# The attention of a hybrid encoder layer as one sequence of steps, two stretches on TensorE for a pair of heads in place of four

## The chip, the cores and the metric

The kernel runs on one core of a Trainium2 chip. A core has five engines that work side by side, each from a queue of its own and in order: TensorE (PE) for matmuls, with the loading of its stationary operand shown apart (PEld); VectorE (DVE) and ScalarE (ACT) for elementwise work; GpSimd (POOL); and SyncE (SP), which here only sends DMAs. Matmul results land in PSUM, eight banks of 128 x 512 float32; everything else lives in SBUF. The metric is the device time of one execution in microseconds.

## What is computed

One encoder layer on 512 tokens (a grid of 8 rows x 64 columns) of width 2048, all in float32. The normalised input goes through one projection. Half of its columns feed a gated depthwise convolution (group A), the other half a neighbourhood attention with 16 heads of width 64 (group B); both are normalised, concatenated, projected and added to the input; then follow a gated MLP with a short convolution and a last normalisation. The part that the change touches is the attention:

```python
def neighborhood_attention(q, k, v, rpb):
    ...
    def row_block(r):
        rs = jnp.clip(r - kh // 2, 0, rows - kh)
        k_rows = lax.dynamic_slice_in_dim(kg, rs, kh, axis=1)
        v_rows = lax.dynamic_slice_in_dim(vg, rs, kh, axis=1)
        k_win = k_rows[:, :, col_idx]
        v_win = v_rows[:, :, col_idx]
        q_row = lax.dynamic_index_in_dim(qg, r, axis=1, keepdims=False)
        scores = jnp.einsum("bchd,bicjhd->bchij", q_row, k_win).astype(jnp.float32)
        dr = rs + jnp.arange(kh) - r + (WIN_H - 1)
        bias = rpb_cols[:, dr]
        scores = scores + jnp.transpose(bias, (2, 0, 1, 3))[None]
        p = jax.nn.softmax(scores.reshape(b, GRID_W, h, kh * kw), axis=-1)
        p = p.reshape(b, GRID_W, h, kh, kw).astype(v.dtype)
        return jnp.einsum("bchij,bicjhd->bchd", p, v_win)
```

A token sees all 8 rows and a window of 16 columns.

## The kernel before

**Projection.** `project(n)` computes 128 columns of the projection for all 512 tokens into one PSUM bank. Each weight unit (8 blocks of 128 x 128) is loaded by SP, split by ACT into a rounded part (`whi`, line 125) and by DVE into the rest (`wlo`, line 126), and each block makes three matmuls in `mm3` (lines 136 to 138): 24 matmuls a unit, two units a column block. The text `ORDER` (line 59) says what is projected when: "a" is two blocks of group A (value and gate), "q" is a pair of heads (its queries and its keys), "v" half of the values of all heads.

**Ticks.** Work other than the projection is written as Python generators in two lists, `steps` and `asteps`. After the last matmul of a unit `tick(m)` advances the first generator of each list by one `yield`, and `issue_after` (line 147) keeps the matmuls so issued behind `m` on TensorE. If a generator ends, the next one of its list starts in the same tick. "a" and "q" make four ticks each, the first "v" sixteen, the second none; the output projection `out_half` makes sixteen for each half. The order on the engines is then made by a planner that takes instructions by priority (which follows the program) as their operands and buffers are ready; `pin` holds an instruction behind the one written just before it on its engine. The first matmul of each part is not pinned.

**Attention.** The heads go in pairs, eight of them. A head's tokens are cut into four column blocks of 16 columns x 8 rows (128 queries), each against 32 columns x 8 rows (256 keys). For each pair `attend` has parts that each treat two blocks of both heads:

- `scores(b0)`: four matmuls (line 452; each stands as two records in the trace), operands of 64 rows, the two heads in the two halves of the array's rows; then on DVE the bias table is added (line 462, the table loaded at line 458 by SP) and the maximum taken, on ACT the exponential (467) and the scaling by the reciprocal sum (470). The scores take the one PSUM tile `sc` of two banks.
- `turn()`: eight transposes (line 482) into the two banks `tr`, copied by ACT to SBUF (`pt`, line 486).
- `values(b0)`: eight matmuls (line 495; two records each), the heads in the two halves of the array's columns, into the one bank `po`. After the second call ACT copies `po` out (`ao`, line 512) and the sum of squares is taken.

A generator for each pair runs them: scores(0) in its first tick, nothing in the second, turn and scores(2) in the third, values(0) in the fourth, turn in the fifth, values(2) in the sixth, in which the next pair's scores(0) follows if that pair is already projected.

**Beside and behind it.** `group_a` (in `asteps`, from the fourth pair on) makes the normalisations of group A; it uses the `tr` banks too. When all pairs are done, `norm_b` normalises group B and splits it into `mbh` and `mbl` (lines 169 and 170). `out_half(ma)` projects group A's half and runs while the last pairs are worked off; `out_half(mb)` needs `mbh` and `mbl`. Most SBUF tiles of 128 x 512 come from one pool `t2k` with 73 slots (`NT`).

Of the kernel before, what the change touches and what calls it, by code (L numbers as in the profile page):

```python
# [10 lines left out]
F32 = mybir.dt.float32  # L11
F32R = mybir.dt.float32r
AF = mybir.ActivationFunctionType
# [3 lines left out]
P = 128  # L17
D = 2048
S = 512
# [13 lines left out]
NP_ = HEADS // 2  # L33
# [4 lines left out]
BLK = 16  # L38
# [36 lines left out]
def layer(ctx: ExitStack, tc: tile.TileContext, xT, w_in, w_v, w_out, w_up, w_down, par, g3r, tab, out):  # L75
    nc = tc.nc
# [6 lines left out]
    psa = ctx.enter_context(tc.tile_pool(name="psa", bufs=1, space=bass.MemoryType.PSUM))  # L83
# [9 lines left out]
    def t2(name, dt=F32):  # L93
        return tp.tile([P, S], dt, tag="t2k", name=name)
# [46 lines left out]
    steps, asteps = [], []  # L141
# [31 lines left out]
    def sum_sq(acc, src, first):  # L173
        if first:
            nc.scalar.activation(acc, src, AF.Square)
        else:
            q = t2("sq")
            nc.scalar.activation(q, src, AF.Square)
            nc.vector.tensor_add(acc, acc, q)
# [72 lines left out]
    for step in ORDER:  # L252
        if step == "v":
            i = next(v_)
# [3 lines left out]
        i = next(a_ if step == "a" else q_)  # L258
# [7 lines left out]
    rstd, late = [], []  # L266
# [13 lines left out]
    def project(n):  # L280
        ps = psm.tile([P, S], F32, tag="mm", name="pj")
        for u in range(KD // U):
            w = weights()
            for k in range(U):
                kk = u * U + k
                m = mm3(ps, w, k, xs[kk][0], xs[kk][1], kk == 0, kk == KD - 1)
                if k % TICK == TICK - 1:
                    tick(m)
            while late and rstd:
                late.pop(0)()  # L290
        return ps
# [3 lines left out]
    def project_values():  # L295

        h = len(vts)
        if h == 0:
            both = psa.tile([P, 2, S], F32, tag="sc", name="pv")
            ps = [both[:, 0], both[:, 1]] + [psm.tile([P, S], F32, tag="mm", name="pv") for _ in range(2)]  # L300
        else:
            while late:
                late.pop(0)()
            ps = ([psa.tile([P, S], F32, tag="tr", name="pv", bufs=2)] +
                  [psm.tile([P, S], F32, tag="mm", name="pv") for _ in range(3)])
        for u in range(KD // 2):
            w = weights()
            for c in range(2):
                kk = 2 * u + c
                a = slice(c * S, (c + 1) * S)  # L310
                for i in range(S // P):
                    xh, xl = (x[:, i * P:(i + 1) * P] for x in xs[kk])
                    nc.tensor.matmul(ps[i], xh, w[0][:, a], start=kk == 0, stop=False)  # L313
                    nc.tensor.matmul(ps[i], xh, w[1][:, a], start=False, stop=False)  # L314
                    m = nc.tensor.matmul(ps[i], xl, w[0][:, a], start=False, stop=kk == KD - 1)  # L315
                if h == 0:
                    tick(m)
            while late and rstd:
                late.pop(0)()
        vd = dram.tile([S, S], F32, name=f"vd{h}")  # L320
        for i in range(S // P):
            t = t2("v")
            nc.scalar.activation(t, ps[i], AF.Copy, scale=rcol[:, i:i + 1])
            nc.sync.dma_start(vd[i * P:(i + 1) * P], t)
        by = vd.rearrange("(r c) d -> r c d", c=GW)
        vt = []
        for b in range(NB):
            for ch in range(2):
                vt.append(t2("vt"))
                for r in range(4):  # L330
                    nc.sync.dma_start(vt[-1][r * KW:(r + 1) * KW], by[4 * ch + r, KC0[b]:KC0[b] + KW])
        vts.append(vt)
# [83 lines left out]
    aos = []  # L416
    acc_na = t2("accna")

    def grid(t, c0, w):
        return t.rearrange("p (r c) -> p r c", c=GW)[:, :, c0:c0 + w]  # L420

    def qkv(p):
        got = []
        for j, nm in enumerate("qk"):
            ps = project(2 * NC_ + j * NP_ + p)
            if nm == "q":

                t = t2(nm)
                by = "p (r b c) -> p r b c"
                nc.vector.tensor_mul(t.rearrange("p (b r c) -> p r b c", b=NB, r=WH),  # L430
                                     ps.rearrange(by, b=NB, r=WH), rstd[0].rearrange(by, b=NB, r=WH))
            else:
                t = t2(nm)
                nc.vector.tensor_mul(t, ps, rstd[0])
            got.append(t)
        return got

    def attend(p, q, k):


        hps = [slice(j * DH, (j + 1) * DH) for j in range(2)]
        vt = vts[p * 2 // NP_]
        cols = [slice(p % (NP_ // 2) * P + j * DH, p % (NP_ // 2) * P + (j + 1) * DH) for j in range(2)]
        po = psa.tile([P, S], F32, tag="po", name="po")
        soft = []

        def scores(b0):
            both = psa.tile([P, 2, 2, 2 * P], F32, tag="sc", name="sc")
            for i in range(2):
                b = b0 + i  # L450
                for j, hp in enumerate(hps):
                    m = nc.tensor.matmul(both[:, j, i, :], q[hp, b * P:(b + 1) * P], grid(k, KC0[b], KW)[hp],
                                         start=True, stop=True)
                    if i or j:
                        pin(m)
            for j in range(2):
                tb = t2("tab").rearrange("p (i k) -> p i k", i=2)
                i = nc.sync.dma_start(tb, tab[2 * p + j][:, b0 // 2:b0 // 2 + 2])
                if p == 0:
                    pin(i)  # L460
                s = t2("s").rearrange("p (i k) -> p i k", i=2)
                nc.vector.scalar_tensor_tensor(s, both[:, j], DH ** -0.5, tb, op0=ALU.mult, op1=ALU.add)
                nm = sm.tile([P, 2], F32, tag="nm", name="nm")
                nc.vector.tensor_reduce(nm, s, axis=AX.X, op=ALU.max, negate=True)
                su = sm.tile([P, 2], F32, tag="su", name="su")
                for i in range(2):
                    nc.scalar.activation(s[:, i], s[:, i], AF.Exp, bias=nm[:, i:i + 1], accum_out=su[:, i:i + 1])
                nc.vector.reciprocal(su, su)
                for i in range(2):
                    nc.scalar.activation(s[:, i], s[:, i], AF.Copy, scale=su[:, i:i + 1])  # L470
                soft.append(s)

        pts = []

        def turn():
            pts.clear()
            for j in range(2):
                s = soft.pop(0)
                ps = psa.tile([P, 4, P], F32, tag="tr", name="trp", bufs=2)
                for i in range(2):  # L480
                    for ch in range(2):
                        m = nc.tensor.transpose(ps[:, 2 * i + ch, :], s[:, i, ch * P:(ch + 1) * P], ident)
                        if i or j or ch:
                            pin(m)
                pt = t2("pt").rearrange("p (c k) -> p c k", c=4)
                nc.scalar.activation(pt, ps, AF.Copy)
                pts.append(pt)

        def values(b0):
            for i in range(2):  # L490
                b = b0 + i
                for ch in range(2):
                    for j in (1, 0):
                        hp = hps[j]
                        m = nc.tensor.matmul(grid(po, b * BLK, BLK)[hp], vt[2 * b + ch][:, cols[j]],
                                             pts[j][:, 2 * i + ch, :], start=(ch == 0), stop=(ch == 1))
                        if (i, ch, j) != (0, 0, 1):
                            pin(m)

        scores(0)  # L500
        yield
        yield
        turn()
        scores(2)
        yield
        values(0)
        yield
        turn()
        yield
        values(2)  # L510
        ao = t2("ao")
        nc.scalar.activation(ao, po, AF.Copy)
        aos.append(ao)
        sum_sq(acc_na, ao, p == 0)

    p, n = -1, 0
    for step in ORDER:
        if step == "v":
            project_values()
            continue  # L520
        if step == "a":
            if n < 2:
                with tc.issue_after(last.ins):
                    glu(n)
            else:
                glu(n)
            n += 1
            continue
        p += 1
        steps.append(attend(p, *qkv(p)))  # L530
        if p == NORM_AT:
            asteps.append(group_a())

# [478 lines left out]
```

## Time and profile before

| | |
|---|---|
| median of 3 runs | 2034.68 us (2034.24 to 2035.8) |
| profiled execution | 2034.49 us |
| span of its instructions | 2032.7 us |
| TensorE busy | 2023.2 us (100%) |
| VectorE busy | 1594.4 us (78%) |
| ScalarE busy | 1035.0 us (51%) |
| mean granted TensorE clock | 0.999 |
| attention on TensorE | first scores at 145.0 us, last values at 558.7 us |

Rows of the timeline read: start in us, duration in us, engine, line of the kernel, operation, output tile <- input tiles, shape of the operands, number of instructions merged into the row. Matmuls are pipelined, so the durations of neighbours overlap, and the distance between two starts says more than a duration. Rows of a tile's view give minimum, median and maximum duration in ns, and the first and the last start in us. Rows of waits read: engine and line <- what it waited for: us in total, times, longest.

### The profile page before, as it was taken

The numbers are of one execution on the slowest core, as the hardware profiler recorded it, in microseconds if no ns is written. First come the engines' busy times: TensorE is split into PE (matmuls) and PEld (weight loads), VectorE is DVE, ScalarE is ACT, GpSimd is POOL, SyncE is SP. The second block draws the span as 40 slices with busy tenths as digits, with TensorE's granted clock in tenths as the row PEclk, the third lists the DMA queues.
The fourth block names the chain that finished last, engine by engine and source line by source line (L and its number), as shares of the span: only waits on it lengthen the run. The fifth ranks groups of instructions, "written<-read, shape, count | busy, mean of one in ns | idle before, by whom it ended". The sixth has DMA issues, their size and how long they took to land.

```text
span 2032.7 us, 27622 instructions
## 1 busy us (share of the span) xinstructions
PE 2023.2 (100%) x10546; PEld 1716.7 (84%) x10546; DVE 1594.4 (78%) x1981; ACT 1035.0 (51%) x1530; POOL 141.6 (7%) x174
## 2 busy tenths in 40 slices
PE   9999999999999999999999999999999999999998
PEld 7888888877888998888888888888888888888887
DVE  7798893876577898787877877877787877888886
ACT  7224423476445645555645645545555645545553
POOL 0000000000001000001101111111110110110000
PEclk9999999999999999999999999999999999999999
DMA  6532325325447544456756666656666656766563
GB/s 235 166 104 83 97 92 175 104 83 178 143 143 178 125 129 141 141 151 150 151 136 165 138 154 144 159 134 159 147 152 142 141 133 142 173 160 163 133 191 133
DMA packets 121189, 293.15 MB, mean 144 GB/s; under 512 B 29408, under 2 KB 29920, under 8 KB 121056
## 3 DMA queue, kind: packets, MB, share of 16 engines
q1 hardware_dynamic: 97296, 246.28, 39.5%
q0 software_dynamic: 23040, 44.05, 14.4%
q8 instruction: 83, 1.36, 0.3%
q10 hardware_dynamic: 720, 1.06, 0.1%
q14 instruction: 50, 0.41, 0.1%
HBM read 232.61 MB, written 58.72 MB: 143 GB/s over the span
## 4 chain that ended last, share of the span: by engine, by line
PE 99%; DMA 0%; DVE 0%; ACT 0%; SPq 0%; issue 0%; DVEq 0%
PE pu L695 14%; PE pv L695 11%; PE pd L794 8%; PE pd L796 8%; PE pd L795 8%; PE pu L702 8%; PE pj L136 6%; PE pj L137 6%; PE pv L702 6%; PE pj L138 6%; PE po L136 3%; PE po L138 3%; PE po L137 3%; PE pv L314 1%; PE pv L315 1%; PE pv L313 1%
## 5 line engine op out<-in xcount | busy, mean ns | idle before, releaser
L125 ACT ACTIVATE whi<-raw 128x1024 fp32r<-128x1024 f32 x364 | 383.5, 1054 | 442.1 <-PE pd L796 172.0
L126 DVE TENSOR_TENSOR wlo<-raw,whi 128x1024 fp32r<-128x1024 f32 x364 | 444.3, 1221 | 171.5 <-ACT whi L125 157.1
L695 PE MATMUL pu<-xc,whi 128*128 128x512 f32 x1280 | 344.8, 391 | 0.0
L695 PEld LDWEIGHTS pu<-xc,whi 128*128 128x128 f32 x1280 | 241.2, 189 | 42.3
L695 PE MATMUL pv<-xc,whi 128*128 128x512 f32 x960 | 259.9, 392 | 0.0
L794 PE MATMUL pd<-whi,hh 128*128 128x512 f32 x640 | 249.9, 391 | 0.0
L796 PE MATMUL pd<-whi,hl 128*128 128x512 f32 x640 | 249.4, 390 | 0.0
L795 PE MATMUL pd<-wlo,hh 128*128 128x512 f32 x640 | 249.1, 389 | 0.0
L695 PEld LDWEIGHTS pv<-xc,whi 128*128 128x128 f32 x960 | 181.3, 189 | 30.9
L125 ACT ACTIVATE whi<-ws 128x1024 fp32r<-128x1024 f32 x132 | 139.8, 1059 | 132.3 <-issue 49.3
L136 PE MATMUL pj<-xh,whi 128*128 128x512 f32 x512 | 200.6, 396 | 0.1
L138 PE MATMUL pj<-xh,wlo 128*128 128x512 f32 x512 | 200.3, 391 | 0.0
L137 PE MATMUL pj<-xl,whi 128*128 128x512 f32 x512 | 200.2, 391 | 0.1
L702 PEld LDWEIGHTS pu<-xc,wlo 128*128 128x128 f32 x1280 | 174.6, 190 | 12.5
L702 PE MATMUL pu<-xc,wlo 128*128 128x256 f32 x1280 | 178.5, 282 | 0.0
L371 DVE SCALAR_TENSOR_TENSOR y<-ch,prm,y 128x507 f32<-128x507 f32 (+14 forms) x240 | 171.5, 741 | 3.4
L126 DVE TENSOR_TENSOR wlo<-ws,whi 128x1024 fp32r<-128x1024 f32 x132 | 161.2, 1221 | 4.5 <-ACT whi L125 4.4
L821 POOL DMA_DIRECT2D xq<-pdc x120 | 104.7, 872 | 828.1 <-ACT pdc L819 820.1
L796 PEld LDWEIGHTS pd<-whi,hl 128*128 128x128 f32 x640 | 120.1, 188 | 26.0
L795 PEld LDWEIGHTS pd<-wlo,hh 128*128 128x128 f32 x640 | 120.2, 188 | 25.8 <-DVE wlo L126 0.3
L794 PEld LDWEIGHTS pd<-whi,hh 128*128 128x128 f32 x640 | 120.5, 188 | 22.0
L702 PEld LDWEIGHTS pv<-xc,wlo 128*128 128x128 f32 x960 | 131.0, 190 | 9.4
(188 smaller groups left out, 3169.3 us busy)
## 6 DMA issues: line engine op xcount, KB each, us to landing
raw<-in_w_up SPq DMA_DIRECT2D x176, 512.0 KB, 3.6
raw<-in_w_down SPq DMA_DIRECT2D x88, 512.0 KB, 3.6
xq<-pdc POOLq DMA_DIRECT2D x136, 256.0 KB, 4.9
raw<-in_w_in SPq DMA_DIRECT2D x60, 512.0 KB, 3.8
raw<-in_w_out SPq DMA_DIRECT2D x32, 512.0 KB, 3.7
x<-in_xT SPq DMA_DIRECT2D x32, 256.0 KB, 5.1
raw<-in_w_v SPq DMA_DIRECT2D x16, 512.0 KB, 4.1
tab<-in_tab SPq DMA_DIRECT2D x32, 256.0 KB, 4.2
```

What stands on the lines that cost most here:

```text
L125: i = nc.scalar.activation(hi[:, :n], raw[:, :n], AF.Copy)
L126: j = nc.vector.tensor_sub(lo[:, :n], raw[:, :n], hi[:, :n].bitcast(F32))
L136: nc.tensor.matmul(ps, hi[:, a], mh, start=start, stop=False)
L137: nc.tensor.matmul(ps, hi[:, a], ml, start=False, stop=False)
L138: return nc.tensor.matmul(ps, lo[:, a], mh, start=False, stop=stop)
L371: nc.vector.scalar_tensor_tensor(y[:, a:b], h[:, a + j - PAD:b + j - PAD], prm[:, o + j:o + j + 1], y[:, a:b], op0=ALU.mult, op1=ALU.add)
L695: return nc.tensor.matmul(to, hi[:, a(k)], comb[c][k], start=first and k == 0, stop=k == U - 1, skip_group_check=not first)
L702: nc.tensor.matmul(to[:, H:], lo[:, a(k)], comb[c][k][:, :H], start=False, stop=False, skip_group_check=not first)
L794: nc.tensor.matmul(ps, h, hi, start=start, stop=False)
L795: nc.tensor.matmul(ps, h, lo, start=False, stop=False)
L796: return nc.tensor.matmul(ps, l, hi, start=False, stop=stop)
L821: nc.gpsimd.dma_start(xq[a][i], t, accum_op=ALU.add)
```

## The change

The generator per pair goes. `pair(p, q, k)` only returns the three functions `scores`, `turn` and `values` of a pair, the transposed tiles are kept under their block number, and the closing copy moves into `values(2)`. One generator `attention()` for all pairs takes them from a list `ready`, to which a pair is added when it has been projected. In its ticks stand, with an empty tick after each: turn(0), scores(2) and the values(2) of the pair before; then values(0), turn(2) and, if the next pair is ready, its scores(0). If it isn't, its scores(0) open a stretch of their own as soon as it is, with the values(2) that are still due.

```diff
-    def attend(p, q, k):
+    def pair(p, q, k):
...
-        po = psa.tile([P, S], F32, tag="po", name="po")
-        soft = []
+        soft, pts, po = [], {}, []
...
-        pts = []
-
-        def turn():
-            pts.clear()
+        def turn(b0):
+            pts[b0] = []
...
-                pts.append(pt)
+                pts[b0].append(pt)
 
         def values(b0):
+            if not po:
+                po.append(psa.tile([P, S], F32, tag="po", name="po"))
...
-        scores(0)
-        yield
-        yield
-        turn()
-        scores(2)
-        yield
-        values(0)
-        yield
-        turn()
-        yield
-        values(2)
-        ao = t2("ao")
-        nc.scalar.activation(ao, po, AF.Copy)
-        aos.append(ao)
-        sum_sq(acc_na, ao, p == 0)
+            if b0:
+                ao = t2("ao")
+                nc.scalar.activation(ao, po[0], AF.Copy)
+                aos.append(ao)
+                sum_sq(acc_na, ao, p == 0)
+
+        return scores, turn, values
+
+    ready = []
+
+    def attention():
+
+        late, now = None, None
+        for p in range(NP_):
+            if now is None:
+                while not ready:
+                    yield
+                now = ready.pop(0)
+                now[0](0)
+                if late:
+                    late[2](2)
+                    late = None
+                yield
+                yield
+            scores, turn, values = now
+            turn(0)
+            scores(2)
+            if late:
+                late[2](2)
+            yield
+            yield
+            values(0)
+            turn(2)
+            late, now = now, ready.pop(0) if ready else None
+            if now:
+                now[0](0)
+            yield
+            yield
+        late[2](2)
...
-        steps.append(attend(p, *qkv(p)))
+        ready.append(pair(p, *qkv(p)))
+        if p == 0:
+            steps.append(attention())
```

More of the change, by code (lines that the diff above doesn't have):

```diff
@@ L494, in values @@
                         hp = hps[j]
-                        m = nc.tensor.matmul(grid(po, b * BLK, BLK)[hp], vt[2 * b + ch][:, cols[j]],
-                                             pts[j][:, 2 * i + ch, :], start=(ch == 0), stop=(ch == 1))
+                        m = nc.tensor.matmul(grid(po[0], b * BLK, BLK)[hp], vt[2 * b + ch][:, cols[j]],
+                                             pts[b0][j][:, 2 * i + ch, :], start=(ch == 0), stop=(ch == 1))
                         if (i, ch, j) != (0, 0, 1):
                             pin(m)
-        scores(0)
-        yield
-        yield
-        turn()
-        scores(2)
-        yield
-        values(0)
-        yield
-        turn()
-        yield
-        values(2)
-        ao = t2("ao")
-        nc.scalar.activation(ao, po, AF.Copy)
-        aos.append(ao)
-        sum_sq(acc_na, ao, p == 0)
+            if b0:
[33 more added lines that the diff above has]
+        late[2](2)
     p, n = -1, 0
```

## The prediction

> **What bounds the kernel now.** I read the page first: the busy times and the chain of waits that ended last.
>
> ```profile
> PE 2023.2 (100%) x10546; PEld 1716.7 (84%) x10546; DVE 1594.4 (78%) x1981; ACT 1035.0 (51%) x1530; POOL 141.6 (7%) x174
> ...
> PE 99%; DMA 0%; DVE 0%; ACT 0%; SPq 0%; issue 0%; DVEq 0%
> ```
>
> TensorE is never without work, and 99% of the chain is its own. So a change to the attention counts only through TensorE: by what its instructions cost between the projection's matmuls, or by a wait put into its queue. The profiled execution took 2034.49 us (1.8 us of it outside its span, the same in the changed kernel), and the median of the three runs is 2034.68 us, 0.2 us above that; I add 0.2 at the end.
>
> A busy TensorE doesn't tell what a stretch of attention costs, as matmuls overlap in the records. I take the starts from the timeline of TensorE instead. First the plain pace, then one stretch of each kind, always from the last projection matmul before it to the second one after it (S are scores, line 452; T are the transposes of `turn`, line 482; V are the values, line 495):
>
> ```profile
> 199.64 0.39 PE L137 MATMUL pj<-xl,whi 128*128 128x512 f32 x1
> ...
> 216.87 0.39 PE L138 MATMUL pj<-xh,wlo 128*128 128x512 f32 x1
> 217.18 1.13 PE L452 MATMUL sc<-k,q 64*128 64x256 f32 x8
> 218.25 0.50 PE L136 MATMUL pj<-xh,whi 128*128 128x512 f32 x1
> 218.58 0.40 PE L137 MATMUL pj<-xl,whi 128*128 128x512 f32 x1
> ```
>
> ```profile
> 229.03 0.40 PE L138 MATMUL pj<-xh,wlo 128*128 128x512 f32 x1
> 229.26 1.04 PE L482 MATMUL trp<-ident,s 128*128 128x128 f32 x8
> 230.23 1.14 PE L452 MATMUL sc<-k,q 64*128 64x256 f32 x8
> 231.30 0.50 PE L136 MATMUL pj<-xh,whi 128*128 128x512 f32 x1
> 231.63 0.40 PE L137 MATMUL pj<-xl,whi 128*128 128x512 f32 x1
> ```
>
> ```profile
> 236.66 0.39 PE L138 MATMUL pj<-xh,wlo 128*128 128x512 f32 x1
> 236.98 1.09 PE L495 MATMUL po<-pt,vt 128*64 128x128 f32 x16
> 238.00 0.50 PE L136 MATMUL pj<-xh,whi 128*128 128x512 f32 x1
> 238.34 0.40 PE L137 MATMUL pj<-xl,whi 128*128 128x512 f32 x1
> ```
>
> ```profile
> 243.34 0.40 PE L138 MATMUL pj<-xh,wlo 128*128 128x512 f32 x1
> 243.58 1.04 PE L482 MATMUL trp<-ident,s 128*128 128x128 f32 x8
> 244.37 0.48 PE L136 MATMUL pj<-xh,whi 128*128 128x512 f32 x1
> 244.69 0.40 PE L137 MATMUL pj<-xl,whi 128*128 128x512 f32 x1
> ```
>
> From 199.64 to 216.87 lie 76 steps of the projection: 0.2267 us each. Two such steps are 0.453 us, and what a stretch takes beyond them is its price:
> S alone: 218.58 - 216.87 - 0.453 = 1.26 us.
> T alone: 244.69 - 243.34 - 0.453 = 0.90 us.
> V alone: 238.34 - 236.66 - 0.453 = 1.23 us.
> T and S together: 231.63 - 229.03 - 0.453 = 2.15 us, where 0.90 + 1.26 = 2.16. Putting these two into one stretch saves nothing: a transpose uses the array in the projection's form (128*128 in the rows, against 64*128 for S and 128*64 for V).
>
> The one combination in which something is saved:
>
> ```profile
> 416.94 0.39 PE L138 MATMUL pj<-xh,wlo 128*128 128x512 f32 x1
> 417.26 1.09 PE L495 MATMUL po<-pt,vt 128*64 128x128 f32 x16
> 418.29 1.14 PE L452 MATMUL sc<-k,q 64*128 64x256 f32 x8
> 419.35 0.50 PE L136 MATMUL pj<-xh,whi 128*128 128x512 f32 x1
> 419.69 0.39 PE L137 MATMUL pj<-xl,whi 128*128 128x512 f32 x1
> ```
>
> ```profile
> 452.76 0.39 PE L138 MATMUL pj<-xh,wlo 128*128 128x512 f32 x1
> 453.08 0.70 PE L452 MATMUL sc<-k,q 64*128 64x256 f32 x2
> 453.71 1.10 PE L495 MATMUL po<-pt,vt 128*64 128x128 f32 x16
> 454.73 1.13 PE L452 MATMUL sc<-k,q 64*128 64x256 f32 x6
> 455.79 0.50 PE L136 MATMUL pj<-xh,whi 128*128 128x512 f32 x1
> 456.13 0.39 PE L137 MATMUL pj<-xl,whi 128*128 128x512 f32 x1
> ```
>
> V directly followed by S costs 419.69 - 416.94 - 0.453 = 2.30 us against 1.23 + 1.26 = 2.49: one way out to the projection and one way in are saved, 0.19 us. The second stretch is the same pair of parts in a bad order: the planner of the queue (it sorts by priority and readiness) let the first score matmul go ahead of the values, so that it stood without its partner of the other 64 rows. It cost 456.13 - 452.76 - 0.453 = 2.92 us, 0.43 more than the two apart.
>
> **The change part by part.** No matmul, activation, vector instruction or DMA is added or removed: eight pairs still have two S, two T and two V each, 2 x (1.26 + 0.90 + 1.23) = 6.78 us a pair, 54.2 us in all. What changes is who stands beside whom. Counting ticks through the code (a projection unit of 24 matmuls each): before, a pair has TS, V, T and V, the last V shared with the next pair's S where that pair is already waiting (only from the fourth pair on). That makes 36 stretches. After, they are 21: the first three pairs and the start of the fourth have S (with the put-off V of the pair before, three times), TS and VT; from then on VTS and TSV take turns, four of each, and VT and V close.
>
> Saved at neighbours: S and V stand side by side at three starts and in four TSV, 7 x 0.19 = 1.33 us. In the four VTS a T lies between. No stretch of before shows V followed by T; above it is bounded by those 0.19 each, 0.76 us in all; below, a loss of as much can't be excluded. I take nothing, by the nearest row (T and S, which neither save nor lose): a T costs its 0.90 wherever it stands, so the way out of V's form should be paid as it is paid to the projection.
> [...]
>
> Given back: before has four S behind V itself. Of those shown, the clean one saves 0.19 and the bad one loses 0.43. A turn in that crowded part was also late and split:
>
> ```profile
> 467.96 0.50 PE L136 MATMUL pj<-xh,whi 128*128 128x512 f32 x1
> 468.51 0.44 PE L482 MATMUL trp<-ident,s 128*128 128x128 f32 x2
> ```
>
> The step to the transposes is 0.55 us, where the second projection matmul after an S came after 0.33 (218.25 to 218.58): the T was waited for, 0.2 us. Taking another clean neighbour as well, before stands at -0.38 + 0.43 + 0.2, about 0.25 us above its 54.2. If after has no such accident, it gains 1.33 + 0.25 = 1.6 us; with the same two accidents again, 0.95. I take 1.3 us.
>
> Moved, and hidden: from the fourth pair on, a pair takes four ticks in place of five, so the softmax work of DVE and ACT comes closer together, and the last values come three ticks (16 us of projection pace) earlier. What waits for those is the second half of the output projection:
>
> ```profile
> L136 PE MATMUL po<-mbh,whi x128: 389/389/389, 593.6 to 680.0; 128*128 128x512 f32 x128
> ```
>
> ```profile
> L169 ACT ACTIVATE mbh<-ao,prm x8: 707/709/727, 568.5 to 583.7; 128x512 fp32r<-128x512 f32 x8
> ```
>
> Its operands are ready 9 us ahead (583.7 + 0.7 against 593.6), so coming earlier brings nothing; if the last values came late instead, 9 us would be covered and every further one would be TensorE's. Each `pt` now lives two ticks instead of one, up to four of the 73 slots of `t2k`; the table loads keep their number (two for each S) but stand elsewhere among the weight loads in SP's queue. I cost both at nothing, as long as the softmax is done when its T comes; if not, the second rival is the price.
>
> **Sum.** 2034.49 - 1.3 = 2033.2, and 0.2 for the median: 2033.4 us, own range 2031.5 to 2035.5. The span would still be TensorE's. A measurement of this kernel can tell about 0.2%, 4.1 us, from no change: 2030.6 to 2038.7.
>
> **The rivals.**
> (A) The change doesn't do what it says on the chip: the planner breaks the stretches again, as it did at 453 and 468 us. If all seven V and S neighbours come out in the bad order, 7 x 0.43 = 3.0 us in place of -1.33, less the 0.25 of before: 2034.7 + 3.0 - 0.25 = 2037.5; with the last ten T (from the fourth pair on) waited for by 0.2 as well, 2039.5. For it: only the first matmul of a part is free to move, and V and S now stand in one tick far more often. Against it: only a late operand or a busy bank makes the planner do so.
> (B) Slower, by one mechanism: the softmax is late at T. TensorE's queue is in order, so if a T waits, the S, the V and all projection behind it wait too. Three rows show the margin and its threat (an activation of the scaling; then from the list of waits, us in total, times, the longest; then the same for SP's queue between 400 and 560 us):
>
> ```profile
> 225.05 1.70 ACT L470 ACTIVATE s<-s,su 128x256 f32<-128x256 f32 x4
> ```
>
> ```profile
> DVE s L462 <- DMA tab<-in_tab: 22.6, 15, 3.0
> ```
>
> ```profile
> SPq L120 <- DVE wlo L126: 82.0, 16, 14.1
> ```
>
> The scaling ends at 226.75, the T starts at 229.26: 2.5 us to spare. But DVE waited 15 times for a table, 1.5 us in the mean, and a table queued behind a weight load on SP can wait longer, as those waited up to 14.1 us for their buffer. In the dense part there are now 10.9 us (two ticks) from the end of an S to its T and no other stretch between. Beyond 2.5 us of lateness every further microsecond is TensorE's own. The last four pairs have eight turns: late by 1.5 us each, 12 us, so 2034.7 - 1.3 + 12 = 2045.4; by half that, 2039.4. I put it at 2042. Against it: the T of before that came late (the step of 0.55 us from 467.96 to 468.51) lost only 0.2 us, since the planner had seen it and put projection ahead.
> (C) More is saved: every stretch that goes saves the 0.19, T or not, 15 x 0.19 = 2.85 us, and the 0.25 goes too: 2034.7 - 3.1 = 2031.6. The T and S row speaks against it. For over 4.1 us each would have to save 0.26.
>
> **How the numbers follow.** Forecast 0.42, A 0.20, B 0.25, C 0.13. Faster by over 0.2%: C with more saved at each stretch than the V and S row shows, 0.08. Slower by over 0.2%: B, and A with the late T as well (0.05), 0.30. Within: 0.62. The range of 2030.5 to 2042 leaves out the lower part of C (0.06) and the upper half of B (0.12).
>
> **What would show it.** In TensorE's timeline: a stretch VTS takes some 3.4 us beyond the pace and TSV some 3.2; if VTS takes 3.2 as well, V to T saves what V to S does, and C gains. Eight-record S groups cut in 2 and 6 or 4 and 4 around V are A. For B, a step of over 0.5 us ahead of the first transpose, and idle time of TensorE released by the scaling on ACT. Wrong altogether would be a difference outside the stretch from 140 to 590 us: then the change moved something that I haven't seen.

## The result, and the profile after

| | before | changed |
|---|---|---|
| median | 2034.68 us (7 runs, 2033.93 to 2035.8) | 2040.75 us (7 runs, 2039.59 to 2042.79) |
| ratio to before | | 1.0029, 95% interval 1.0020 to 1.0039 |
| span of the profiled execution | 2032.7 us | 2039.0 us |

The changed kernel is slower by 6.1 us, 0.29%, where 1.3 us faster was forecast. The page of the changed kernel, in the rows that were shown of before:

```profile
PE 2025.2 (99%) x10546; PEld 1719.5 (84%) x10546; DVE 1594.1 (78%) x1981; ACT 1035.8 (51%) x1532; POOL 141.3 (7%) x174
...
PE 96%; ACT 2%; DMA 1%; DVE 1%; issue 0%; SPq 0%; DVEq 0%; ACTq 0%
```

The work is the same but for two more instructions on ACT, and the chain of waits that ended last now runs 2% through ACT, 1% through DMA and 1% through DVE, where before TensorE alone had 99%. The whole difference arises before the second half of the output projection; the first matmul of that half starts at 599.9 us, 6.3 us later than the 593.6 of before, and nothing is lost or won behind it:

```profile
L136 PE MATMUL po<-mbh,whi x128: 389/389/389, 599.9 to 686.2; 128*128 128x512 f32 x128
```

The stretches themselves came out as they were reckoned. TensorE's timeline of the changed kernel:

```profile
241.86 0.39 PE L138 MATMUL pj<-xh,wlo 128*128 128x512 f32 x1
242.17 1.09 PE L495 MATMUL po<-pt,vt 128*64 128x128 f32 x16
243.20 1.09 PE L480 MATMUL trp<-ident,s 128*128 128x128 f32 x8
...
244.36 0.40 PE L137 MATMUL pj<-xl,whi 128*128 128x512 f32 x1
...
422.42 0.39 PE L138 MATMUL pj<-xh,wlo 128*128 128x512 f32 x1
422.65 1.03 PE L480 MATMUL trp<-ident,s 128*128 128x128 f32 x8
423.62 1.13 PE L452 MATMUL sc<-k,q 64*128 64x256 f32 x8
424.68 1.09 PE L495 MATMUL po<-pt,vt 128*64 128x128 f32 x16
...
426.04 0.40 PE L137 MATMUL pj<-xl,whi 128*128 128x512 f32 x1
```

V followed by T costs 244.36 - 241.86 - 0.453 = 2.05 us against 1.23 + 0.90 = 2.13 apart, so 0.08 is saved of the 0 to 0.19 that was left open. TSV costs 426.04 - 422.42 - 0.453 = 3.17 against 3.39: 0.22 saved, as with V and S. Then, at the sixth pair, TensorE stands still. The two longest of its waits from 430 to 600 us, and the places in its timeline:

```profile
PE po L495 <- ACT ao L501: 2.8, 1, 2.8
PE trp L480 <- ACT s L470: 1.1, 1, 1.1
```

```profile
478.07 1.97 PE L495 MATMUL po<-pt,vt 128*64 128x128 f32 x16 [2.81 <-ACT ao L501]
...
512.85 0.83 PE L480 MATMUL trp<-ident,s 128*128 128x128 f32 x4 [1.11 <-ACT s L470]
```

The sixth pair's values wait for the bank `po`, which ACT has still to copy out (`ao`) for the fifth pair, though the fifth pair's values were done at 457 us. And the values themselves take 1.97 us in place of 1.09, at a lower granted clock, as the windows of the same kernel show (busy time with instructions in brackets for PE, PEld, DVE, ACT, POOL, then the granted clock):

```profile
474.00:478.00 4.00, 1.27 (x6) 0.73 (x4) 3.02 (x5) 3.89 (x8) 0.00 (x0) 0.96 0.66 161
478.00:482.00 4.00, 3.92 (x25) 3.42 (x26) 0.86 (x2) 4.00 (x12) 0.00 (x0) 0.61 0.27 105
```

For 4 us after the wait TensorE was granted 0.61 of its clock, by estimate 4 x 0.39 = 1.6 us more. Behind it the stretches come apart: counted in TensorE's rows, as runs of attention matmuls between projection matmuls, the changed kernel has 28 stretches and not 21, and all seven additional ones lie behind 475 us.

What ACT did in place of the copy stands in its timeline. Line 467 is the attention's exponential, line 402 group A's swish; each switch between the two loads a function table for 1.28 us:

```profile
446.41 0.57 ACT L210 ACTIVATE rln<-st 128x512 f32<-128x512 f32 x1
447.69 0.91 ACT L470 ACTIVATE s<-s,su 128x256 f32<-128x256 f32 x2 [0.71 <-DVE su L468]
448.62 1.28 ACT L402 ACT_TABLE_LOAD   x1
449.92 0.82 ACT L402 ACTIVATE y<-y,prm 128x512 f32<-128x512 f32 x1
450.75 1.28 ACT L467 ACT_TABLE_LOAD   x1
...
454.58 1.28 ACT L402 ACT_TABLE_LOAD   x1
...
464.51 1.05 ACT L125 ACTIVATE whi<-raw 128x1024 fp32r<-128x1024 f32 x1
...
474.08 1.06 ACT L125 ACTIVATE whi<-raw 128x1024 fp32r<-128x1024 f32 x1 [1.66 <-DMA raw<-in_w_out]
475.15 1.28 ACT L467 ACT_TABLE_LOAD   x1
...
477.45 0.57 ACT L501 ACTIVATE ao<-po 128x512 f32<-128x512 f32 x1
```

And SP's timeline beside it:

```profile
444.08 23.09 SPq L120 DMA_DIRECT2D raw<-in_w_in  x2
467.26 0.38 SPq L458 DMA_DIRECT2D tab<-in_tab  x1
```

The first of these rows merges two weight loads. One went out at 444.08; the other stood at the head of SP's queue until its buffer came free, and was the longest of SP's waits (between 380 and 600 us, in the form of the rows of waits):

```profile
SPq L120 <- DVE wlo L126: 165.3, 29, 20.6
```

Read backwards: the copy at 477.45 stands on ACT behind the exponentials of the sixth pair's second scores, as `scores(2)` is written ahead of the put-off `values(2)`. Those exponentials need a table that SP sent only at 467.26, behind the weight load that had waited 20.6 us. The next weight load (469.24) was sent behind that table, and ACT stood idle for it too before it came to the exponentials (the 1.66 us at 474.08). The buffer came free only when ACT, at 464.51, and then DVE had split the weights in it; and ACT came to that only after group A's eight swishes. These began late and were cut in two, because the exponentials of the sixth pair's first scores, which now stand in the same tick as the matmul that releases the swishes (`rln`, 446.41), went in between. Half of these exponentials were late for a reason of the same kind. Their table went out behind another weight load that had waited for its buffer. In the profile's chain of waits (start, duration, what) it is sent at 442.55, and DVE adds it at 446.89:

```profile
442.55 4.32 DMA tab<-in_tab
446.89 0.69 DVE s L462
```

The view of line 402 in both kernels (durations in ns, first and last start in us):

```profile
L402 ACT ACTIVATE y<-y,prm x8: 802/804/817, 445.0 to 454.6; 128x512 f32<-128x512 f32 x8
```

```profile
L402 ACT ACTIVATE y<-y,prm x8: 799/803/817, 449.9 to 463.2; 128x512 f32<-128x512 f32 x8
```

The last swish starts at 454.6 before and at 463.2 in the changed kernel, 8.6 us later.

### The profile page after: what moved, and what is told of

It is laid out like the page before. It is cut to its first block, busy times and chain, and to the rows that moved or that the text cites. A ratio compares the mean times of both kernels' runs of the same rounds, so it can differ in the third digit from the quotient of the medians.

```text
span 2039.0 us, 27621 instructions
## 1 busy us (share of the span) xinstructions
PE 2025.2 (99%) x10546; PEld 1719.5 (84%) x10546; DVE 1594.1 (78%) x1981; ACT 1035.8 (51%) x1532; POOL 141.3 (7%) x174
## 4 chain that ended last, share of the span: by engine, by line
PE 96%; ACT 2%; DMA 1%; DVE 1%; issue 0%; SPq 0%; DVEq 0%; ACTq 0%
PE pu L720 14%; PE pv L720 11%; PE pd L819 8%; PE pd L821 8%; PE pd L820 8%; PE pu L727 7%; PE pv L727 6%; PE pj L136 5%; PE pj L137 5%; PE pj L138 5%; PE po L136 3%; PE po L137 3%; PE po L138 3%; PE pv L314 1%; PE pv L313 1%; PE pv L315 1%
## 5 line engine op out<-in xcount | busy, mean ns | idle before, releaser
L371 DVE SCALAR_TENSOR_TENSOR y<-ch,prm,y 128x499 f32<-128x499 f32 (+14 forms) x240 | 171.7, 740 | 3.5
```

Of the source, the lines that this page charges most:

```text
L371: nc.vector.scalar_tensor_tensor(y[:, a:b], h[:, a + j - PAD:b + j - PAD], prm[:, o + j:o + j + 1], y[:, a:b], op0=ALU.mult, op1=ALU.add)
```

## The experiments

The kernel before, timed beside these runs, has a median of 2034.86 us (beside the last four runs 2034.76), and the ratios are to that.

**The order within a stretch.**

```diff
             turn(0)
-            scores(2)
             if late:
                 late[2](2)
+            scores(2)
```

> Edit: in the changed kernel the put-off values(2) are written before scores(2), so that the copy out of the values bank gets ahead of the exponentials of scores(2) on ACT. Order theory (the 2.8 us wait of the values at 475 us for that copy is the main loss): that wait goes, the stretches become T V S, 2037.5 us (2040.75 less 2.9). Density theory (four ticks for a pair leave the softmax too little time, and the wait for the bank is only the place where it is felt): the loss shows at a transpose instead, 2039.5 to 2041.

Measured: 2037.35 us, ratio 1.0015 (1.0006 to 1.0024). The copy now ran at 464.81, and the wait for the bank was gone, but another took its place:

```profile
PE trp L480 <- ACT s L470: 3.6, 3, 2.5
```

The time is that of the order theory, the trace that of the density theory: the loss moved to a transpose, which waits for late exponentials and their scaling (2.5 us at 473, and no reduced clock behind it: 1.00 in the windows from 470 to 482 us). The swishes are in one piece here, but end late all the same (the last starts at 460.0). So the order alone is not the cause.

**Five ticks for a pair.**

```diff
             yield
             yield
+            if p < NP_ - 1:
+                yield
         late[2](2)
```

> Edit: in the changed kernel one more empty tick for each pair but the last, so five ticks a pair as before the change, with the same two stretches. Density theory: the waits on TensorE (2.8 us at 475, 1.1 at 511 and some of 0.3) go, and the saving of 1.3 us at the neighbours is left: 2033 to 2035 us. Order theory: the copy still stands behind the exponentials, and half of the loss or more stays: 2037 to 2040. Slot theory (the transposed tiles live longer and starve the pool of 73 slots): they live longer still here, 2040 or more.

Measured: 2033.17 us, ratio 0.9991 (0.9982 to 1.0000), 7.6 us under the changed kernel with the same two stretches for a pair. No wait for a bank or a transpose is left from 430 to 600 us:

```profile
PE st L208 <- DVE dg L205: 0.8, 1, 0.8
PE st L196 <- ACT pt L484: 0.4, 1, 0.4
```

The two that remain are matmuls of group A's statistics. The transposed tiles live longer here than in the changed kernel, so their hold on the pool isn't what cost the time.

**Three stretches, five ticks.** One generator for each pair again, in place of `attention()` (only the lines that come in are shown):

```diff
+    def attend(p, q, k):
+        scores, turn, values = pair(p, q, k)
+        scores(0)
+        yield
+        yield
+        turn(0)
+        scores(2)
+        yield
+        yield
+        values(0)
+        turn(2)
+        yield
+        values(2)
```

> Edit: one generator for each pair again, with the changed kernel's functions: scores(0); two ticks; turn(0), scores(2); two ticks; values(0), turn(2); one tick; values(2) and the next pair's scores(0). Three stretches for a pair, five ticks. Density theory: 2033.5 to 2035.5 us, no wait of over 0.5 us on TensorE. Order theory: values(2) are ahead of the next scores here, so also near before, 2034 to 2036. Slot theory: the transposed tiles of values(0) live two ticks as in the changed kernel, 2037 or more.

Measured: 2035.93 us (2034.57 to 2038.15), ratio 1.0005 (0.9996 to 1.0014): not to be told from before. TensorE has no wait for the attention, but one of 1.6 us of group A's statistics for DVE (in its profiled execution, which was the slowest of its eleven). The density theory's figure is missed by 0.4 us, and so is its bound of 0.5 us for any wait, though none is the attention's; the order theory's 2034 to 2036 holds it. So this run doesn't tell the two apart.

**A bank of its own for the sixth and eighth pair.**

```diff
-                po.append(psa.tile([P, S], F32, tag="po", name="po"))
+                po.append(psa.tile([P, S], F32, tag="po", name="po") if p not in (5, 7) else
+                          psm.tile([P, S], F32, tag="mm", name="po"))
```

> Edit: in the changed kernel the values of the sixth and the eighth pair go to a bank of the projection's three, so that the values(0) that waited at 475 us have a bank of their own; the order stays. Bank theory: the wait of 2.8 us goes and nothing takes its place, 2037.5 us. Density theory: behind that bank the transposes wait for the same late exponentials, 2 us or more come back at the next transpose, 2039.5 to 2041. If one bank fewer holds up the projection, that shows as a wait of a matmul of line 136 for DVE.

Measured: 2048.3 us, ratio 1.0065 (1.0052 to 1.0077), worse than either theory had it. The wait for the copy is gone, and the late exponentials are waited for at transposes, as the density theory said; but the bank was also missing elsewhere, where scores now wait for the keys:

```profile
PE trp L480 <- ACT s L470: 5.4, 4, 3.5
PE sc L452 <- DVE k L434: 4.3, 2, 4.0
```

```profile
490.00:494.00 4.00, 4.00 (x11) 3.23 (x12) 1.98 (x7) 2.28 (x5) 0.00 (x0) 0.50 0.63 215
```

From 486 to 494 us TensorE was busy for 3.61 + 4.00 us at a granted clock of 0.50; by estimate that adds 8 x 0.50, some 4 us, of its own. The run shows that the bank was not the root, and no more.

**Four ticks without the merging.** Only the lines that come in are shown:

```diff
+            turn(0)
+            scores(2)
+            yield
+            values(0)
+            yield
+            turn(2)
+            now = ready.pop(0) if ready else None
+            if now:
+                now[0](0)
+            yield
+            values(2)
+            if now:
+                yield
```

> Edit: four ticks for a pair as in the changed kernel, but not its merging: turn(0) and scores(2); values(0); turn(2) and the next pair's scores(0); values(2), each in a tick of its own, four stretches for a pair. Density theory: slower than before by what the waits cost there, 2036.5 to 2041 us, with waits on TensorE of over 1 us in all between 437 and 525 us. Merging theory (the parts that stand behind one another in a stretch make the loss): no wait beyond those of before, 2034 to 2035.5.

Measured: 2044.09 us, ratio 1.0047 (1.0033 to 1.0060), 9 us over before, 3 over the changed kernel and 3 over the density theory's upper figure. The waits are again those for the exponentials (4.1 us in three), and again the clock fell behind the longest:

```profile
PE trp L480 <- ACT s L470: 4.1, 3, 2.8
```

```profile
524.00:527.00 3.00, 3.00 (x8) 2.28 (x8) 1.39 (x2) 1.26 (x3) 0.00 (x0) 0.52 0.74 249
```

So four ticks for each of the last five pairs cost the time without the merging as well, and the kernel that merges is the faster of the two.

**One more tick behind the fourth and the fifth pair only.**

```diff
             yield
             yield
+            if p in (3, 4):
+                yield
         late[2](2)
```

> Edit: the changed kernel with one more empty tick behind the fourth and the fifth pair only; the sixth to the eighth keep four ticks. If the crowding is that of the softmax with the work of group A alone (its last matmuls at about 500 us): as with five ticks throughout, 2033 to 2034 us. If four ticks are too few in any case: half of the gain or less, 2036 to 2039.

Measured: 2033.06 us, ratio 0.9991 (0.9982 to 1.0000). The sixth to the eighth pair run at four ticks here and lose nothing: as far as these two kernels tell, four ticks are too few only beside group A's work. The swishes stand in one piece on ACT, and the weights behind them are split at 453.38, 11 us earlier than in the changed kernel:

```profile
L402 ACT ACTIVATE y<-y,prm x8: 798/800/814, 444.3 to 452.7; 128x512 f32<-128x512 f32 x8
```

**The same with the other order of the parts.** Five ticks as above, and `values(2)` written ahead of `scores(2)`.

> Edit: five ticks for a pair but the last, and the put-off values(2) written before scores(2). If the order matters only where the softmax is late: no change against five ticks alone, 2032.7 to 2033.7 us. If the copy out of the bank has a cost of its own there too: 2031.5 to 2032.5.

Measured: 2033.54 us, ratio 0.9993 (0.9984 to 1.0001): no change. The order matters only where the softmax is late.

**The tables by another queue.**

```diff
-                i = nc.sync.dma_start(tb, tab[2 * p + j][:, b0 // 2:b0 // 2 + 2])
+                i = nc.gpsimd.dma_start(tb, tab[2 * p + j][:, b0 // 2:b0 // 2 + 2])
```

> Edit: the changed kernel with the 32 table loads sent by POOL in place of SP, so that none stands behind a weight load that waits for its buffer. If the table (behind a weight load of 23 us on SP's queue, at 444 us) is what makes the softmax late: 2034 to 2036 us, and DVE's waits for tables fall from 18.3 us to under 5. If ACT's own queue is (the eight activations of group A with their table switches, and the weights behind them): 2039 to 2042, with DVE's waits gone all the same.

Measured: 2037.64 us, ratio 1.0012 (1.0003 to 1.0021), between the two figures. The lists of waits, DVE's between 380 and 600 us and TensorE's from 60 to 720 us:

```profile
DVE s L462 <- DMA tab<-in_tab: 0.7, 1, 0.7
```

```profile
PE pj L136 <- ACT whi L125: 2.3, 2, 2.1
PE trp L480 <- ACT s L470: 0.2, 1, 0.2
```

DVE's 18.3 us of waiting for tables went to 0.7, and TensorE's waits for the bank and for the exponentials went with them but for 0.2 us. The time is spoilt by a new wait of 2.1 us for split weights, from 333.4 to 335.4 us, and a granted clock of 0.52 behind it, from 337 to 340 us. Two points that both kernels pass separate the two losses: one projection matmul, and the start of the output projection's second half; first the changed kernel's row, then two of this one:

```profile
381.10 0.39 PE L138 MATMUL pj<-xh,wlo 128*128 128x512 f32 x1
```

```profile
385.24 0.39 PE L138 MATMUL pj<-xh,wlo 128*128 128x512 f32 x1
```

```profile
L136 PE MATMUL po<-mbh,whi x128: 389/389/389, 596.7 to 683.1; 128*128 128x512 f32 x128
```

Up to that stretch it is 385.24 - 381.10 = 4.1 us behind, and at the second half of the output projection 3.2 us ahead of the changed kernel's 599.9: between them it gains 7.3 us, nearly the whole loss of 7.7, though the ticks are those of the changed kernel. The swishes are in one piece here. Their last start, 460.7, is late only because the whole kernel runs 4.1 us behind: on the changed kernel's clock it is 460.7 - 4.1 = 456.6, 6.6 us earlier than there. So the tables' place behind weight loads on SP's queue works at both ends of the chain. In the changed kernel it makes the sixth pair's first exponentials so late that they cut the swishes in two, and it holds up that pair's second scores. For the same reason this run can't tell how much the swishes' lateness would cost by itself.

**Where the one tick is needed.** `if p == 3: yield` and `if p == 4: yield` in the same place.

> Edit: the changed kernel with one more empty tick in all, behind the fourth pair's values(0): the fifth pair's turn(0) and all behind it come one tick later, and every S but the fifth pair's first keeps its two ticks to its T. If a shift of one tick against group A is enough: 2033 to 2034.5 us. If the fifth and sixth pair's softmax need more time while ACT works off group A's eight activations: 2036 to 2040.

Measured: 2034.95 us, ratio 0.9998 (0.9989 to 1.0007), 0.45 us above the first figure. No bank and no transpose is waited for.

> Edit: the same one tick, behind the fifth pair's values(0): the sixth pair's first scores, written in the tick in which group A's activations begin, get three ticks to their T in place of two. If those scores are what comes late: 2033 to 2034.5 us. If the phase against group A before them matters as well: 2035.5 to 2039.

Measured: 2038.67 us, ratio 1.0019 (1.0010 to 1.0028), with the wait for the bank still there:

```profile
PE po L495 <- ACT ao L501: 2.5, 1, 2.5
```

One tick behind the fourth pair takes back 5.8 us, the one a pair later only 2.1, though it gives the sixth pair's first scores more time. So it isn't the way from those scores to their transposes that was too short. With the tables on SP's queue, the sixth pair's first scores must not fall into the tick in which group A's normalisation ends and its swishes begin; with the tables on POOL's they fall there and cost nothing. With the tick behind the fourth pair the last swish starts at 452.7, with the one behind the fifth at 463.2, as in the changed kernel.

**Without the switches of the function table.** This kernel leaves out the swish of group A:

```diff
-            nc.scalar.activation(ys[i], ys[i], AF.Silu, scale=pc("lng", i), bias=pc("lnb", i))
+            nc.scalar.activation(ys[i], ys[i], AF.Identity, scale=pc("lng", i), bias=pc("lnb", i))
```

> Edit: in the changed kernel group A's eight activations (line 402) compute scale times input plus bias, without the swish, which ACT does without loading another function table; the output isn't the reference's. If the two extra table loads (1.28 us each) and the order that they bring are the loss: 2033.5 to 2036 us. If the eight activations and their splits hold up the weights and the softmax by their own 11 us of work: 2038.5 to 2041.

Measured: 2036.44 us, ratio 1.0007 (0.9998 to 1.0015), 4.3 us under the changed kernel but 3.3 over that with five ticks. The wait for the bank is still there, 2.0 us. The result lies 0.4 us above the first figure. The edit takes away the switch that before has too, beside the two additional ones, so 4.3 us is at most what the cut into two pieces and its switches cost. Without them the last of the eight still starts at 458.4, 4 us later than before; this delay is left, and so are the 3.3 us.

**Both: a tick behind the fourth and fifth pair, and the tables by POOL.**

> Edit: the changed kernel with one more empty tick behind the fourth and the fifth pair, and the table loads sent by POOL. If DVE's waits for tables cost nothing any more once the softmax has time: 2032.5 to 2033.6 us, as without the move. If they still do: 2030.5 to 2032.

Measured: 2036.82 us, ratio 1.0007 (0.9998 to 1.0016), a miss for both figures. The waits for split weights, 2.3 us in two, the longer 2.1, came with the move of the tables, as in the run without the ticks; the rest of the 3.8 us to the 2033.06 of the two ticks alone was not taken apart.

## Why the prediction was wrong

**What bounds the kernel, and the prices: right.** TensorE's own rows gave the price of each stretch to some 0.1 us. The three kernels whose rows show the 21 stretches that were counted, or 22, without a loss elsewhere (2033.06, 2033.17 and, with the values first, 2033.54) lie 1.8, 1.7 and 1.3 us under the before of their runs (2034.86), where 1.3 us had been worked out from seven neighbours. V and T, left open and taken at nothing, saves 0.08 each. The working counted it in the four VTS only, but V stands before T in the four VT as well: eight times 0.08, 0.6 us. Rival (C) did not happen.

**The step that failed** is "Moved, and hidden": "I cost both at nothing, as long as the softmax is done when its T comes". "Both" are the longer life of the transposed tiles, rightly put at nothing, and the place of the table loads in SP's queue; with them the closer pace of the last five pairs went at nothing too. The condition, that the softmax is done in time, rested on a margin (2.5 us between scaling and T) taken at the second pair, at 226 us. There ACT has little other work than the attention and the weights: of group A two gates and one table load, 2.6 us in the 36 us of that pair. At 440 to 475 us, where the pace changes, group A's statistics, swishes and splits stand on the same engine, and the row for that margin should have been taken there. The runs show in its place 7.7 us: 2040.75 less 2033.06, which the same stretches take with one more tick at two places. In the profiled execution 2.8 us of it are the wait for the bank, 1.6 us, by estimate, the clock of 0.61 behind it and 1.1 us the later wait of a transpose. Only 0.3 us of waits are left on TensorE's list besides; the other 2.2 us, to which the broken groups behind 475 us belong, were not taken apart.

**Rival (B) named the right mechanism, and missed its place.** It said that the softmax comes late at T, by the tables behind weight loads on SP's queue; it reckoned with eight turns late by 0.75 to 1.5 us each, 2039.4 to 2045.4 us, chose 2042 and gave it 0.25. The lateness was real, and the table at 467.26, behind a weight load that had waited 20.6 us, is a link of it. But the main loss came at one place, not at every turn, and TensorE felt it first at the values, whose bank was held. That its price lies near the measured 2040.75 is luck. Neither the forecast nor the rival looked at ACT's other work.

**What the runs put in its place** is one number of ACT, the start of group A's last swish, against the time:

| kernel | last swish starts, us | median, us |
|---|---|---|
| tick behind the fourth and fifth pair | 452.7 | 2033.06 |
| tick behind the fourth pair | 452.7 | 2034.95 |
| five ticks | 453.0 | 2033.17 |
| five ticks, values first | 453.6 | 2033.54 |
| before | 454.6 | 2034.68 |
| three stretches, five ticks | 456.5 | 2035.93 |
| no swish in it | 458.4 | 2036.44 |
| values first | 460.0 | 2037.35 |
| changed | 463.2 | 2040.75 |
| tick behind the fifth pair | 463.2 | 2038.67 |
| four ticks, four stretches | 464.2 | 2044.09 |

Left out are the three kernels with a loss at another place as well: the values' banks, and the two with the tables by POOL. The starts are of one profiled execution each (with three stretches it was the slowest of eleven, 2038.15 us), the medians of all. From 456 us on a later end of the swishes goes with a longer time, but for two kernels with the same 463.2 that lie 2.1 us apart; below it the times lie within 1.9 us in no such order. What was moved one at a time takes back: the phase 5.8 to 7.7 us, the tables' queue 7.3 at its stage, the table switches at most 4.3, the order of the copy 3.4. These overlap, and their sum means nothing. The phase and the tables' place in SP's queue had to meet: with either of them moved, most or all of the loss is gone. What isn't shown is a share for the swishes' lateness alone, as the run with the tables elsewhere took most of that away too. The changed kernel has two table loads for the swishes where before has one; the kernel with the values first also has one, and waits of 3.6 us for the exponentials all the same, so that keeping the swishes in one piece isn't enough. Why the planner let the late exponentials in between the first swish and the second is not shown; both became ready in one tick.

**Rival (A)**, broken groups, did happen too: up to 475 us the changed kernel's groups are whole, behind it few are, and 13 stretches stand where 6 were counted. No run prices this by itself. The kernel with a tick behind the fourth pair has 26 stretches, waits for no bank and no transpose, and is 1.9 us slower than the one with 21; the kernel with the tables on POOL has 30 and loses hardly anything at that stage. So the size of this term stays open.

## What to carry to other kernels

Where a step sequence is shortened, the steps move against everything else that keeps its own clock: the margin of a wait has to be read at the stage where the new phase meets other work on the same engines, not where the sequence runs alone. A merge of stretches and a closer pace are two changes; done with one more tick at two places, the merge is worth 0.09% (interval 0 to 0.18%; 2033.06 against 2034.86 us), and four ticks without the merge cost 0.47% at the phase that they have here. Here a weight load that waited 20.6 us for its buffer on SP's queue held up the table behind it, which was needed first: what waits and what is urgent belong on different queues. And a copy that frees a bank belongs, in the program, ahead of work that may wait: that was worth 3.4 us in the changed kernel and nothing where the softmax was in time.

## What the hardware showed beside it

Behind some of TensorE's waits the windows show a lower granted clock, soon after the wait or a few us later: 0.61 from 478 to 482 us behind the 2.8 us in the changed kernel, which ended at 478.07; 0.92 and 0.52 from 521 to 524 and from 524 to 527 us behind the 2.8 us with four ticks alone, which ended at 521.15; 1.00 from 335 to 337 and 0.52 from 337 to 340 us behind the 2.1 us with the tables on POOL, which ended at 335.44; and 0.50 from 482 to 494 us with a bank of its own, where the longest waits are 4.0 and 3.5 us. Another wait of 2.5 us, with the values first, left the clock at 1.00 from 470 to 482 us. So what such a wait costs in all can't be told from its length: in the changed kernel 2.8 us became, with the estimated 1.6, 4.4. What sets the clock back was not shown.
